# Both output projections of a decoder layer, formed from seven products of half size

## The chip, the cores and the metric

The program runs on one core of a Trainium2 chip. The metric is the device time of one execution in microseconds (us); a kernel's time is the median of its runs.

## The reference

One decoder layer works on x, 1024 tokens by 1024 features in float32. Four steps follow one another, each with a residual and a LayerNorm:

```
x <- LN1(alpha*x + 1/2 * SwiGLU_1(x))
x <- LN2(alpha*x + concat[HGRN2(x), SGU(x)] @ w_out)
x <- LN3(alpha*x + attention(x, LN_m(mem)) @ xa_w_o)
x <- LN4(alpha*x + 1/2 * SwiGLU_2(x))
```

SwiGLU is `(silu(x @ w_gate) * (x @ w_up)) @ w_down` with 2816 inner features. The two products that this case is about are those with `w_out` and with `xa_w_o`: each multiplies a 1024 x 1024 matrix of activations by a 1024 x 1024 weight.

## The kernel before

**Products.** The work is tiled by 128: eight token tiles, eight k-tiles (of the contraction), and halves of 512 tokens or 512 columns. A float32 operand is split into two parts of a shorter float type: `split` has ScalarE copy the high part, and VectorE subtract it from the operand for the low part (L110). `mm3` then makes each product as three matmuls of 128x512, high by high (L131), high by low (L132) and low by high (L133); The activations that a stage multiplies stand transposed, features on the partitions, in four tiles: `xh` and `xl`, high and low, one pair for each half of the tokens.

**The output projections.** `down_group` (L226) computes a group of token tiles: (0, 1), then (2, 3, 4), then (5, 6, 7). A token tile needs two banks, one for each 512 columns. For each of eight k-tiles a group loads 128 rows of the weight, splits them and multiplies, so the weight is loaded and split three times, 24 loads and 24 splits for each projection. A group has 96 or 144 matmuls, the projection 384. When a group ends, `residual_norm` (L214) is started for each of its tiles: it loads the residual, adds the banks onto it (L220), norms the row on VectorE (two halves of statistics, an aggregate, two passes of 128x1024; the reciprocal root on GpSimd), stores the result, and transposes it into `xh` and `xl` for the next stage.

**Order.** Such later work is a coroutine: `spawn` starts it, it yields a time in us, and `tick` goes on with it once so much time of other products has been issued; `drain` ends all of them. So the norms and transposes of a group stand among the matmuls of the next group or stage. In the mixers (L1056 to L1066) the first group is issued, then the last part of the second half of the tokens (`m1.tail()`, four token tiles of the gate's product, whose transposes complete the second half of the mixers' output), then a drain, then the other two groups. Behind them the attention's first query projection (`paq0`, all of the first half's tokens) begins. In the attention the first group of `xa_w_o` is dealt out among the heads of the second half of the tokens, and the other two groups follow; behind them FFN 2 multiplies its first pair of feature tiles. For FFN 2 the transposed output is also kept in float32 (`keep`, tiles `xf_xa`), because FFN 2 forms combinations of it.

**Buffers and engines.** Weights pass through pools of 3 (raw), 6 (high) and 5 (low) buffers; larger temporary tiles come from one pool of 22 of 128x1024; PSUM has six banks for products and two for transposes. A scheduler sets each engine's order when the program is built, and each engine then works through its own queue in that order. SP issues the transfers.

## Time and profile before

| what | value |
|---|---|
| three runs | 2034.47, 2040.79 (the median) and 2042.2 us |
| span of the profiled execution | 2032.8 us |
| TensorE (PE) busy | 2015.5 us in 9646 matmuls |
| VectorE (DVE) busy | 1504.1 us in 2246 instructions |
| ScalarE (ACT) busy | 890.0 us in 1239 instructions |
| GpSimd (POOL) busy | 102.5 us in 144 instructions |

The profiled execution is one of its own; its span, from its first instruction to its last, is the only time known of it, and stands 8.0 us below the median of the three runs.

The profile gives, for each engine, the time in which it is busy; the rows by stretch give the same between two moments of the span, with the granted TensorE clock and the share in which the transfers ran. Matmuls are pipelined, so that one's duration reaches into the next one's; what a matmul takes of TensorE's time is the distance between two starts. A row of one instruction gives start, duration, engine, line, operation, output <- inputs (without buffer numbers) and shapes.

### The profile page before, as it was taken

The page shows a single profiled execution, that of the slowest core. Times are in us where ns is not written, and L with a number is a line of the kernel's source. Part 1 is how long each engine was busy: PE and PEld are TensorE (multiplying, and loading weights), DVE is VectorE, ACT ScalarE, POOL GpSimd, SP SyncE. Part 2 cuts the span into 40 slices and gives each one's busy share as a digit, 9 for nine tenths or more (in the row PEclk, how much of TensorE's full clock was granted, in tenths as well). Part 3 has the DMA queues.
Part 4 walks back from the last instruction along what each step waited for, and adds up shares of the span by engine and source line. Part 5 has one row for each costly group of instructions (what it writes and reads, how often), then busy time and mean ns, then how long its engine had stood idle before and what let it go on. Part 6 is the DMA issues. An engine that isn't in the chain of part 4 may idle for free.

```text
span 2032.8 us, 25339 instructions
## 1 busy us (share of the span) xinstructions
PE 2015.5 (99%) x9646; PEld 1689.1 (83%) x9646; DVE 1504.1 (74%) x2246; ACT 890.0 (44%) x1239; POOL 102.5 (5%) x144
## 2 busy tenths in 40 slices
PE   8999999999999999999999999999999999999998
PEld 7888888888888888888888888888888888888886
DVE  5987677677668967948796855678776776776688
ACT  6633333334533467547644344444333333344432
POOL 0000000000002010100110100010000000000021
PEclk8999999999999999999999999999999999999999
DMA  8333233237887632123156522353232332378874
GB/s 263 122 114 119 78 114 119 78 119 250 290 289 261 222 116 73 53 63 105 41 176 228 162 88 74 122 197 119 88 126 82 104 127 81 109 249 291 297 254 172
DMA packets 244250, 306.88 MB, mean 151 GB/s; under 512 B 14368, under 2 KB 154272, under 8 KB 244128
## 3 DMA queue, kind: packets, MB, share of 16 engines
q1 hardware_dynamic: 244128, 305.26, 45.3%
q8 instruction: 76, 1.25, 0.2%
q14 instruction: 46, 0.38, 0.1%
HBM read 234.44 MB, written 70.78 MB: 150 GB/s over the span
## 4 chain that ended last, share of the span: by engine, by line
PE 93%; DVE 3%; DMA 2%; POOL 1%; issue 1%; SPq 0%; ACT 0%; POOLq 0%; DVEq 0%; ACTq 0%
PE st_gf L131 7%; PE st_uf L131 7%; PE st_gf L133 7%; PE st_uf L133 7%; PE st_gf L132 7%; PE st_uf L132 7%; PE dp_f L133 6%; PE dp_f L131 6%; PE dp_f L132 6%; PE psl L939 2%; PE acc_xa L131 1%; PE acc_xa L133 1%; PE acc_xa L132 1%; PE paq L131 1%; PE paq L133 1%; PE paq L132 1%
## 5 line engine op out<-in xcount | busy, mean ns | idle before, releaser
L132 PE MATMUL dp_f<-wd_f_l,ah_f 128*128 128x512 f32 x552 | 213.3, 390 | 0.0
L131 PE MATMUL dp_f<-wd_f_h,ah_f 128*128 128x512 f32 x552 | 208.4, 390 | 0.0
L133 PE MATMUL dp_f<-wd_f_h,al_f 128*128 128x512 f32 x552 | 206.1, 390 | 0.1
L133 PEld LDWEIGHTS dp_f<-wd_f_h,al_f 128*128 128x128 f32 x552 | 103.7, 188 | 22.2 <-DVE al_f L110 0.9
L132 PEld LDWEIGHTS dp_f<-wd_f_l,ah_f 128*128 128x128 f32 x552 | 103.6, 188 | 21.6
L131 PEld LDWEIGHTS dp_f<-wd_f_h,ah_f 128*128 128x128 f32 x552 | 103.6, 188 | 21.2
L109 ACT ACTIVATE wd_f_h<-wd_f_r 128x1024 fp32r<-128x1024 f32 x72 | 73.2, 1022 | 97.7 <-DVE wd_f_r L436 28.3
L110 DVE TENSOR_TENSOR al_f<-ar_f,ah_f 128x1024 fp32r<-128x1024 f32 x72 | 84.5, 1174 | 24.5 <-ACT ah_f L109 23.6
L109 ACT ACTIVATE ah_f<-ar_f 128x1024 fp32r<-128x1024 f32 x72 | 73.3, 1019 | 59.2 <-DMA ar_f<-lops 54.3
L110 DVE TENSOR_TENSOR wd_f_l<-wd_f_r,wd_f_h 128x1024 fp32r<-128x1024 f32 x72 | 84.3, 1175 | 12.5 <-ACT wd_f_h L109 12.2
L316 DVE TENSOR_TENSOR top_uf<-bot_uf,st_uf 128x512 f32<-128x512 f32 x21 | 14.4, 686 | 81.8 <-PE st_uf L133 81.8
L315 ACT ACTIVATE bot_gf<-st_gf 128x512 f32<-128x512 f32 x21 | 12.5, 597 | 137.1 <-PE st_gf L133 137.1
L560 POOL TENSOR_SCALAR nm_f<-nm_f 128x1 f32<-128x1 f32 x8 | 10.7, 1336 | 1198.8 <-ACT xl L559 1198.8
L131 PE MATMUL st_gf<-xh,wg_f_h 128*128 128x512 f32 x168 | 65.4, 389 | 0.0
L133 PE MATMUL st_gf<-xh,wg_f_l 128*128 128x512 f32 x168 | 65.4, 389 | 0.0
L131 PE MATMUL st_uf<-xh,wu_f_h 128*128 128x512 f32 x168 | 65.4, 389 | 0.0
L132 PE MATMUL st_uf<-xl,wu_f_h 128*128 128x512 f32 x168 | 65.4, 389 | 0.0
L133 PE MATMUL st_uf<-xh,wu_f_l 128*128 128x512 f32 x168 | 65.4, 389 | 0.0
L132 PE MATMUL st_gf<-xl,wg_f_h 128*128 128x512 f32 x168 | 65.3, 389 | 0.0
L109 ACT ACTIVATE wg_f_h<-wg_f_r 128x1024 fp32r<-128x1024 f32 x44 | 46.4, 1056 | 36.2 <-PE st_gf L132 29.3
L109 ACT ACTIVATE wu_f_h<-wu_f_r 128x1024 fp32r<-128x1024 f32 x44 | 46.3, 1053 | 35.7 <-issue 27.2
L110 DVE TENSOR_TENSOR wu_f_l<-wu_f_r,wu_f_h 128x1024 fp32r<-128x1024 f32 x44 | 53.6, 1219 | 3.2 <-PE acc_xa L132 3.2
(456 smaller groups left out, 5960.1 us busy)
## 6 DMA issues: line engine op xcount, KB each, us to landing
ar_f<-lops SPq DMA_DIRECT2D x66, 512.0 KB, 5.0
wd_f_r<-in_ffn_w_down_dram SPq DMA_DIRECT2D x56, 512.0 KB, 4.8
wg_f_r<-in_ffn_w_gate_dram SPq DMA_DIRECT2D x44, 512.0 KB, 3.8
wu_f_r<-in_ffn_w_up_dram SPq DMA_DIRECT2D x44, 512.0 KB, 3.8
wd_mx_r<-in_w_out_dram SPq DMA_DIRECT2D x24, 512.0 KB, 3.6
wd_xa_r<-in_xa_w_o_dram SPq DMA_DIRECT2D x24, 512.0 KB, 3.5
lops<-bot_gf SPq DMA_DIRECT2D x21, 512.0 KB, 2.7
lops<-top_uf SPq DMA_DIRECT2D x21, 512.0 KB, 2.8
```

Source lines behind the costliest of these rows:

```text
L109: order(nc.scalar.activation(hi, src, AF.Copy))
L110: order(nc.vector.tensor_tensor(lo, src, hi.bitcast(F32), op=ALU.subtract))
L131: nc.tensor.matmul(ps, lh, rh, start=first, stop=False)
L132: nc.tensor.matmul(ps, lh, rl, start=False, stop=False)
L133: nc.tensor.matmul(ps, ll, rh, start=False, stop=last)
L315: nc.scalar.activation(b0, product(1), AF.Copy)
L316: nc.vector.tensor_tensor(t0, b0, product(2), op=ALU.add)
L560: nc.gpsimd.tensor_scalar(nmean, nmean, -1.0 / D, None, op0=ALU.mult)
L939: nc.tensor.matmul(psl[:m, (i * NC2 + c) * 64:(i * NC2 + c + 1) * 64] .rearrange("p (n b) -> p n b", b=B), e[:, :m], blk(e, B)[:, :, 1, :] ...
```

## The change

`square` takes the place of `down_group` and `residual_norm` for both projections. It halves the tokens (rows of blocks), the contraction and the columns, and forms the product of the resulting 2x2 blocks from seven products of blocks instead of eight. With a11, a12, a21, a22 for the activations' blocks (first index: half of the tokens, second: half of k) and w11 to w22 for the weight's:

```
t1 = w12 - w11    t2 = w22 - t1    s1 = a21 + a22    s2 = s1 - a11
p1 = a11 w11      p2 = a12 w21     p5 = s1 t1        p6 = s2 t2
p3 = (a12 - s2) w22    p7 = (a11 - a21)(w22 - w12)    p4 = a22 (w21 - t2)
top left  = p1 + p2              top right    = p1 + p6 + p5 + p3
bottom left = p1 + p6 + p7 + p4  bottom right = p1 + p6 + p7 + p5
```

The products run in the order 1, 2, 5, 6, 3, 7, 4. Each has four token tiles and four k-tiles, 48 matmuls, so a projection has 336. Products 1 and 2 end in the banks `sx`, 5 and then 3 are accumulated in `sz`, and 6, 7 and 4 in `sy`; `mm3` got an argument for a bank that is accumulated on after it was read. `top` and `bot` are the residuals of the first and second four token tiles, onto which the banks are added one after the other (`onto`). VectorE forms the weight's combinations (`right`) and the activations' (`plus`), and the operands that are not blocks of the input are split again. The norms of the tiles of `top` are started after product 3, those of `bot` tile by tile in product 4, and `square` ends by completing the coroutines of `top` at once.

Since combinations need the float32 blocks, the mixers and the attention now write their transposed output to float32 tiles (`oa`, `ao`). For the first half of the tokens it is also split into `xh` and `xl`, stored to DRAM, and loaded again (`mx_again`, `ao_again`) when products 5, 6 and 3 need it. In the mixers, `m1.tail()` now comes ahead of the whole projection, four steps of the projection (products 1 and 2) are issued behind it, then the drain, then the rest; in the attention, products 1 and 2 are dealt out among the heads. 

```diff
-    def mm3(ps, lh, ll, rh, rl, first, last):
+    def mm3(ps, lh, ll, rh, rl, first, last, more=False):
...
+    def square(w, left, res_src, gb, bb, dst, name, keep=None):
+        wv = w.rearrange("(kb n i p) (db d) -> kb n db p i d", kb=2, n=2, i=2, p=P, db=2)
+        early = []
+        def block(kb, db, n, of):
+            return load_raw(wv[kb, n, db], f"w{of}_{name}_{n}")
+        def kept(kb, db, n, of):
+            return load_raw(wv[kb, n, db], f"w{of}_{name}_{n}", gt)
+        def plus(a, b, op, o=None):
+            nc.vector.tensor_tensor(a if o is None else o, a, b, op=op)
+            return a if o is None else o
+        t1, t2, b22 = {}, {}, {}
+        def right(p, n):
+            if p == 1:
+                r = block(0, 0, n, p)
+            elif p == 2:
+                r = block(1, 0, n, p)
+            elif p == 5:
+                r = kept(0, 1, n, p)
+                t1[n] = plus(r, block(0, 0, n, "5b"), ALU.subtract)
+            elif p == 6:
+                b22[n] = kept(1, 1, n, p)
+                t2[n] = r = plus(b22[n], t1[n], ALU.subtract, t1[n])
+            elif p == 3:
+                r = b22[n]
+            elif p == 7:
+                r = block(0, 1, n, p)
+                plus(b22[n], r, ALU.subtract, r)
+            else:
+                r = plus(block(1, 0, n, p), t2[n], ALU.subtract)
+            return split_w(r, f"w{p}_{name}_{n}")
+        def product(p, bank, slot, first, done=None):
+            half, k0 = slot
+            ops = [right(p, 0)]
+            def part(t, n):
+                ts = slice(t * P, (t + 1) * P)
+                rh, rl = ops[n]
+                for i in range(2):
+                    k = k0 + 2 * n + i
+                    mm3(bank[t], xh[half][:, k, ts], xl[half][:, k, ts], rh[:, i, :], rl[:, i, :],
+                        first and n == 0 and i == 0, n == 1 and i == 1, not first)
+            if done is None:
+                for n in range(2):
+                    if n == 0:
+                        ops.append(right(p, 1))
+                    for t in range(4):
+                        part(t, n)
+                    yield 5.4
+                return
+            ops.append(right(p, 1))
+            for t in range(4):
+                for n in range(2):
+                    part(t, n)
+                done(t)
+                yield 2.7
+        def residual(tt):
+            r = gt(f"r_{name}_{tt}", (P, 2, HALF))
+            nc.sync.dma_start(r, res_src[tt * P:(tt + 1) * P, :].rearrange("p (h d) -> p h d", h=2))
+            return r
+        def onto(r, acc, scale=None):
+            if scale is None:
+                nc.vector.tensor_tensor(r, r, acc, op=ALU.add)
+            else:
+                nc.vector.scalar_tensor_tensor(r, r, scale, acc, op0=ALU.mult, op1=ALU.add)
+        def norm(r, tt, lag):
+            y = r.rearrange("p h d -> p (h d)")
+            layer_norm(y, gb, bb, f"{name}_{tt}")
+            nc.sync.dma_start(dst[tt * P:(tt + 1) * P, :], y)
+            yield lag
+            yield from to_xT_steps(y, tt, list(range(KT)), f"{name}_{tt}", keep, 2.6)
+        x = [ps_mm(f"sx_{name}_{t}") for t in range(4)]
+        yield from product(1, x, (0, 0), True)
+        p1 = [gt(f"p1_{name}_{i}", (P, 2, HALF)) for i in range(2)]
+        p1 = [p1[t // 2][:, t % 2, :] for t in range(4)]
+        for t in range(4):
+            nc.scalar.activation(p1[t], x[t], AF.Copy)
+        yield from product(2, x, (0, 4), False)
+        top = [residual(t) for t in range(4)]
+        for t in range(4):
+            onto(top[t][:, 0], x[t], ALPHA)
+        s1, a11, a12, a21, a22 = {}, {}, {}, {}, {}
+        for n in range(2):
+            a21[n], a22[n] = left(1, 0, n), left(1, 1, n)
+            s1[n] = plus(a21[n], a22[n], ALU.add, gt(f"s1_{name}_{n}", (P, 2, HALF)))
+            ks = slice(2 * n, 2 * n + 2)
+            split(s1[n], xh[1][:, ks, :], xl[1][:, ks, :])
+        z = [(ps_tr if t > 1 else ps_mm)(f"sz_{name}_{t}") for t in range(4)]
+        yield from product(5, z, (1, 0), True)
+        for n in range(2):
+            a11[n] = left(0, 0, n)
+            ks = slice(2 * n, 2 * n + 2)
+            plus(a11[n], a21[n], ALU.subtract, a21[n])
+            plus(s1[n], a11[n], ALU.subtract)
+            split(s1[n], xh[0][:, ks, :], xl[0][:, ks, :])
+        for t in range(4):
+            onto(top[t][:, 1], p1[t], ALPHA)
+        bot = [residual(4 + t) for t in range(4)]
+        for t in range(4):
+            onto(bot[t][:, 1], z[t], ALPHA)
+        y = [ps_mm(f"sy_{name}_{t}") for t in range(4)]
+        yield from product(6, y, (0, 0), True)
+        for n in range(2):
+            ks = slice(4 + 2 * n, 6 + 2 * n)
+            a12[n] = left(0, 1, n)
+            plus(a12[n], s1[n], ALU.subtract)
+            split(a12[n], xh[0][:, ks, :], xl[0][:, ks, :])
+        for t in range(4):
+            onto(top[t][:, 1], y[t])
+            onto(bot[t][:, 0], p1[t], ALPHA)
+        yield from product(3, z, (0, 4), False)
+        for n in range(2):
+            ks = slice(2 * n, 2 * n + 2)
+            split(a21[n], xh[1][:, ks, :], xl[1][:, ks, :])
+        for t in range(4):
+            onto(top[t][:, 1], z[t])
+            early.append(norm(top[t], t, 6 + 4.5 * t))
+            spawn(early[-1])
+            onto(bot[t][:, 1], p1[t])
+        yield from product(7, y, (1, 0), False)
+        for n in range(2):
+            ks = slice(4 + 2 * n, 6 + 2 * n)
+            split(a22[n], xh[1][:, ks, :], xl[1][:, ks, :])
+        for t in range(4):
+            onto(bot[t][:, 1], y[t])
+        def done(t):
+            onto(bot[t][:, 0], y[t])
+            spawn(norm(bot[t], 4 + t, 8))
+        yield from product(4, y, (1, 4), False, done)
+        for f in [f for f in flows if f[0] in early]:
+            flows.remove(f)
+            for _ in f[0]:
+                pass
...
+            cs = slice(i * P, (i + 1) * P)
+            for j in range(2):
+                if i == 0:
+                    self.oa[j] = gt(f"oaT{self.half}{j}", (P, 2, HALF))
+                nc.scalar.activation(self.oa[j][:, :, cs], ptv[:, 2 * j:2 * j + 2, :], AF.Copy)
+            if self.half:
+                return
+            split(ptv, xh[0][:, 0:4, cs], xl[0][:, 0:4, cs])
             if i == NC2 - 1:
                 for j in range(2):
                     ks = slice(4 + 2 * j, 6 + 2 * j)
-                    split(self.u[j], xh[self.half][:, ks, :], xl[self.half][:, ks, :])
+                    split(self.u[j], xh[0][:, ks, :], xl[0][:, ks, :])
+                    nc.sync.dma_start(oa_dram[0, j], self.oa[j])
+                    nc.sync.dma_start(oa_dram[1, j], self.u[j])
...
-    def mix_group(grp):
-        return down_group(a["w_out"][0], KT, grp, xT_operand, res[0], gb, bb, res[1], "mx")
-    run(mix_group((0, 1)))
+    def mixed(i, j, n):
+        if i:
+            return (m1.u if j else m1.oa)[n]
+        a32 = gt(f"mx_again_{j}{n}", (P, 2, HALF))
+        nc.sync.dma_start(a32, oa_dram[j, n])
+        return a32
+    project = square(a["w_out"][0], mixed, res[0], gb, bb, res[1], "mx")
     play(m1.tail())
+    for _ in range(4):
+        tick(next(project))
     drain()
-    run(mix_group((2, 3, 4)))
-    run(mix_group((5, 6, 7)))
+    run(project)
...
+        ao = gt(f"ao{half}_{h}", (P, 2, HALF))
         for j in range(2):
             c = h * 2 + j
             cs = slice(c * P, (c + 1) * P)
...
-            split(ps, xh[half][:, c, :], xl[half][:, c, :])
+            nc.scalar.activation(ao[:, j, :], ps, AF.Copy)
+        if half:
+            aos[h] = ao
+        else:
+            split(ao, xh[0][:, 2 * h:2 * h + 2, :], xl[0][:, 2 * h:2 * h + 2, :])
+            nc.sync.dma_start(ao_dram[h], ao)
...
+    project = square(a["xa_w_o"][0], attended, res[1], gb, bb, res[2], "xa", xf2)
     for h in range(H):
         if h:
-            next(first)
+            tick(next(project))
         probs_T(1, h)
         if h < H - 1:
             scores(1, h + 1)
         else:
-            next(first)
-        next(first)
+            tick(next(project))
         attend(1, h)
-    run(first)
-    run(out_group((2, 3, 4)))
-    run(out_group((5, 6, 7)))
+    run(project)
```

The first place is VectorE's queue in the mixers' projection, where the last tile of the second half of the mixers' output (`ot11`) has been gated. Before, there stood the gating, the splits of normed tiles of the first group (`xl0<-pt_mx`), those of the second group's weights (`wd_mx`) and of the mixers' second half (`xl1<-ut`):

```order
L875 TENSOR_TENSOR ot11_7751<-ot11_7751,sg12_8720 128x512
L110 TENSOR_TENSOR xl0_117<-pt_mx_1_0_8723,xh0_115 128x4x128
L110 TENSOR_TENSOR xl0_117<-pt_mx_1_4_8730,xh0_115 128x4x128
L110 TENSOR_TENSOR wd_mx_2_1_l_8830<-wd_mx_2_1_r_8827,wd_mx_2_1_h_8829 128x1024
L110 TENSOR_TENSOR wd_mx_2_2_l_8854<-wd_mx_2_2_r_8851,wd_mx_2_2_h_8853 128x1024
L110 TENSOR_TENSOR wd_mx_2_3_l_8878<-wd_mx_2_3_r_8875,wd_mx_2_3_h_8877 128x1024
L110 TENSOR_TENSOR xl1_118<-ut10_7433,xh1_116 128x1024
```

In the changed kernel, after s1 has been formed and split, the residuals `r_mx`, the bank of products 1 and 2 (`sx`), the kept product 1 (`p1`), the combinations for product 5 (`w5`) and those of the activations (`oaT`, reloaded as `mx_again`) stand in this order:

```order
L296 SCALAR_TENSOR_TENSOR r_mx_3_8739<-r_mx_3_8739,sx_mx_3_8541 128x512
L296 SCALAR_TENSOR_TENSOR r_mx_3_8739<-r_mx_3_8739,p1_mx_1_8638 128x512
L235 TENSOR_TENSOR w5_mx_0_r_8757<-w5_mx_0_r_8757,w5b_mx_0_r_8759 128x1024
L235 TENSOR_TENSOR w5_mx_1_r_8766<-w5_mx_1_r_8766,w5b_mx_1_r_8768 128x1024
L235 TENSOR_TENSOR oaT10_8708<-mx_again_00_8823,oaT10_8708 128x1024
L235 TENSOR_TENSOR s1_mx_0_8745<-s1_mx_0_8745,mx_again_00_8823 128x1024
L235 TENSOR_TENSOR oaT11_8710<-mx_again_01_8829,oaT11_8710 128x1024
L235 TENSOR_TENSOR s1_mx_1_8749<-s1_mx_1_8749,mx_again_01_8829 128x1024
L296 SCALAR_TENSOR_TENSOR r_mx_4_8839<-r_mx_4_8839,p1_mx_0_8637 128x512
L110 TENSOR_TENSOR w5_mx_0_l_8763<-w5_mx_0_r_8757,w5_mx_0_h_8762 128x1024
L296 SCALAR_TENSOR_TENSOR r_mx_5_8841<-r_mx_5_8841,p1_mx_0_8637 128x512
L110 TENSOR_TENSOR w5_mx_1_l_8772<-w5_mx_1_r_8766,w5_mx_1_h_8771 128x1024
```

The split of product 5's weights (`w5_mx_0_l`) now stands behind residual additions and combinations for product 6.

The second place is TensorE's queue between the end of the mixers' projection and the first query projection (`paq0`). Before, one followed the other (`acc_mx` are the banks of the projection):

```order
L131 MATMUL acc_mx_7_1_9048<-wd_mx_5_7_h_9261,xh1_116 128x512
L132 MATMUL acc_mx_7_1_9048<-wd_mx_5_7_l_9262,xh1_116 128x512
L133 MATMUL acc_mx_7_1_9048<-wd_mx_5_7_h_9261,xl1_118 128x512
L131 MATMUL paq0_0_9361<-xh0_115,waq0_0_h_9357 128x512
L132 MATMUL paq0_0_9361<-xl0_117,waq0_0_h_9357 128x512
L133 MATMUL paq0_0_9361<-xh0_115,waq0_0_l_9358 128x512
```

Now (`pt_mx_t_j` are the transposes of half j of token tile t of the projection's normed output, four to a row):

```order
L159 MATMUL pt_mx_2_4_9245<-ident_75,r_mx_2_8737 128x128 x4
L159 MATMUL pt_mx_4_0_9252<-ident_75,r_mx_4_8839 128x128 x4
L159 MATMUL pt_mx_3_0_9284<-ident_75,r_mx_3_8739 128x128 x4
L132 MATMUL paq0_0_9342<-xh0_115,waq0_0_h_9338 128x512
L132 MATMUL paq0_1_9398<-xh0_115,waq0_1_h_9394 128x512
L132 MATMUL paq0_2_9445<-xh0_115,waq0_2_h_9441 128x512
L132 MATMUL paq0_3_9480<-xh0_115,waq0_3_h_9476 128x512
L132 MATMUL paq0_4_9513<-xh0_115,waq0_4_h_9509 128x512
L132 MATMUL paq0_5_9548<-xh0_115,waq0_5_h_9544 128x512
L159 MATMUL pt_mx_4_4_9291<-ident_75,r_mx_4_8839 128x128 x4
L159 MATMUL pt_mx_5_0_9298<-ident_75,r_mx_5_8841 128x128 x4
L133 MATMUL paq0_0_9342<-xl0_117,waq0_0_h_9338 128x512
```

Transposes of four tiles, and six matmuls on high parts alone, now stand ahead of the first matmul on a low part, which needs tiles 0 to 3 normed and split.

The third place is the same queue between the attention's projection and FFN 2 (`pg_f2` and `pu_f2` are its first products). Before:

```order
L131 MATMUL acc_xa_7_1_11048<-wd_xa_5_7_h_11289,xh1_116 128x512
L132 MATMUL acc_xa_7_1_11048<-wd_xa_5_7_l_11290,xh1_116 128x512
L133 MATMUL acc_xa_7_1_11048<-wd_xa_5_7_h_11289,xl1_118 128x512
L131 MATMUL pg_f2_0_0_11366<-xh0_115,wg_f2_0_h_11362 128x512
L132 MATMUL pg_f2_0_0_11366<-xl0_117,wg_f2_0_h_11362 128x512
L133 MATMUL pg_f2_0_0_11366<-xh0_115,wg_f2_0_l_11363 128x512
```

Now:

```order
L159 MATMUL pt_xa_2_0_11177<-ident_75,r_xa_2_10681 128x128 x4
L159 MATMUL pt_xa_2_4_11213<-ident_75,r_xa_2_10681 128x128 x4
L159 MATMUL pt_xa_4_0_11224<-ident_75,r_xa_4_10783 128x128 x4
L159 MATMUL pt_xa_3_0_11262<-ident_75,r_xa_3_10683 128x128 x4
L159 MATMUL pt_xa_4_4_11273<-ident_75,r_xa_4_10783 128x128 x4
L132 MATMUL pg_f2_0_0_11315<-xh0_115,wg_f2_0_h_11311 128x512
L132 MATMUL pu_f2_0_0_11379<-xh0_115,wu_f2_0_h_11375 128x512
L132 MATMUL pg_f2_1_0_11435<-xh0_115,wg_f2_1_h_11431 128x512
L132 MATMUL pu_f2_1_0_11466<-xh0_115,wu_f2_1_h_11462 128x512
L159 MATMUL pt_xa_5_0_11286<-ident_75,r_xa_5_10785 128x128 x4
L159 MATMUL pt_xa_3_4_11297<-ident_75,r_xa_3_10683 128x128 x4
L133 MATMUL pg_f2_0_0_11315<-xl0_117,wg_f2_0_h_11311 128x512
```

Here too the transposes of tiles 2 to 5 and four matmuls on high parts stand between the projection and the first low part.

52 lines of the change are left out of this document (18 added, 34 removed).

## The prediction

> **What bounds the kernel now.** I read the page's busy table and its chain of waits first, then stretches around the two projections, then single instructions there.
>
> ```profile
> span 2032.8 us, 25339 instructions
> PE 2015.5 (99%) x9646; PEld 1689.1 (83%) x9646; DVE 1504.1 (74%) x2246; ACT 890.0 (44%) x1239; POOL 102.5 (5%) x144
> PE 93%; DVE 3%; DMA 2%; POOL 1%; issue 1%; SPq 0%; ACT 0%; POOLq 0%; DVEq 0%; ACTq 0%
> 1020.00:1060.00 40.00, 39.58 (x238) 34.32 (x236) 37.20 (x89) 19.35 (x27) 3.62 (x6) 1.00 0.57 196
> 1060.00:1100.00 40.00, 40.00 (x210) 33.99 (x209) 27.14 (x39) 16.07 (x29) 4.13 (x5) 1.00 0.54 202
> 1100.00:1150.00 50.00, 50.00 (x234) 41.58 (x233) 38.39 (x45) 20.95 (x23) 5.40 (x6) 1.00 0.60 196
> 1150.00:1190.00 40.00, 40.00 (x191) 33.35 (x190) 30.15 (x40) 13.59 (x19) 3.46 (x6) 1.00 0.42 132
> sum 170.00, PE 169.58 PEld 143.24 DVE 132.87 ACT 69.95 POOL 16.62; mean PE 42.39 PEld 35.81 DVE 33.22 ACT 17.49 POOL 4.15
> sum 125.00, PE 125.00 PEld 104.74 DVE 92.42 ACT 52.89 POOL 13.62; mean PE 41.67 PEld 34.91 DVE 30.81 ACT 17.63 POOL 4.54
> ```
>
> The first three lines are the page's: TensorE is busy 99% of the span and makes 93% of the chain. The others give busy time by stretch (PE, PEld, DVE, ACT, POOL, then the clock). The mixers' projection with its surroundings is 1020 to 1190: PE lost 0.42 us there, and VectorE, the next in line, was free for 170 - 132.9 = 37.1 us. The last line sums 1275 to 1400, around the attention's projection: PE lost nothing, VectorE was free for 32.6 us. So every matmul that goes shortens the run, as long as VectorE keeps up.
>
> **What the change removes.** Each projection had 384 matmuls and now has 7/8 of them, 336; the instruction order shows 96 fewer over the program. Their price is the distance between starts, not the 0.39 us that one takes:
>
> ```profile
> 1101.78 0.39 PE L131 MATMUL acc_mx<-wd_mx_h,xh 128*128 128x512 f32 x1
> ...
> 1107.90 0.39 PE L131 MATMUL acc_mx<-wd_mx_h,xh 128*128 128x512 f32 x1
> 1068.80 0.87 PE pt_mx L158 x8
> ```
>
> From the first to the last of these rows there are 27 starts in 6.12 us: 0.2267 us each. The removal is worth 96 x 0.2267 = **21.8 us**, all of it on the path. A transpose costs 0.87 / 8 = 0.109 us.
>
> **What it adds.** By the order, VectorE gets 34 more instructions of 128x1024 and 20 more of 128x512. Their prices are again distances between starts, from stretches in which VectorE did not pause:
>
> ```profile
> 1154.03 1.22 DVE L110 TENSOR_TENSOR waq_l<-waq_r,waq_h 128x1024 fp32r<-128x1024 f32 x1
> 1155.16 0.68 DVE L220 SCALAR_TENSOR_TENSOR r_mx<-r_mx,acc_mx 128x512 f32<-128x512 f32 x1
> 1155.76 0.20 DVE L196 BATCH_NORM_AGGREGATE mv_mx<-st_mx 128x2 f32<-128x12 f32 x1
> 1156.00 1.28 DVE L202 SCALAR_TENSOR_TENSOR r_mx<-r_mx,mv_mx,g_mx 128x1024 f32<-128x1024 f32 x1
> 1157.20 1.28 DVE L192 BATCH_NORM_STATS2 st_mx<-r_mx 128x6 f32<-128x512 f32 x2
> 1158.40 1.27 DVE L204 SCALAR_TENSOR_TENSOR r_mx<-r_mx,rs_mx,b_mx 128x1024 f32<-128x1024 f32 x1
> 1159.58 1.22 DVE L110 TENSOR_TENSOR waq_l<-waq_r,waq_h 128x1024 fp32r<-128x1024 f32 x1
> ...
> 1420.31 1.22 DVE L270 TENSOR_TENSOR xf_xa<-xf_xa,xf_xa 128x1024 f32<-128x1024 f32 x1
> 1421.45 1.22 DVE L110 TENSOR_TENSOR xc6l_f<-xf_xa,xc6h_f 128x1024 fp32r<-128x1024 f32 x1
> 1428.85 0.68 DVE L286 TENSOR_TENSOR wu_f_sa<-wu_f_sa,wu_f_r 128x512 f32<-128x512 f32 x1
> 1429.45 0.69 DVE L287 TENSOR_TENSOR wu_f_r<-wu_f_r,wu_f_r 128x512 f32<-128x512 f32 x1
> 1400.81 1.43 DVE L110 TENSOR_TENSOR xl<-xf_xa,xh 128x256 fp32r<-128x256 f32 x4
> 1402.15 0.68 DVE L285 TENSOR_TENSOR wg_f_sa<-wg_f_r 128x512 f32<-128x512 f32 x1
> ```
>
> A plain 128x1024 operation costs 1.13 to 1.14 us, a 128x512 one or half of the statistics 0.60, the LayerNorm's 128x1024 steps 1.20 and 1.18 (I take 1.19), the aggregate 0.24, a 128x256 split 1.34 / 4 = 0.335. The addition is 34 x 1.135 + 20 x 0.60 = 50.6 us, 25.3 for each projection. By totals that would just fit: 37.1 - 10.9 = 26.2 us are left free at the mixers. But VectorE works in order, so what counts is what stands in its queue between the moment when s1 can be formed and the moment when the next stage has its operand. I count rows of the order.
>
> At the **mixers**, the queue from s1_mx_0 to the split of pt_mx_3_0 (xl for the first k-tiles of the fourth token tile, which the first query projection reads whole) holds 119 instructions: 43 plain 128x1024 (48.8 us), 58 of 128x512 or statistics (34.8), 6 aggregates (1.4), 12 LayerNorm steps (14.3), **99.3 us** together. On the way, the low part of product 5's first weights comes after 18.5 us and that of product 6's after 34.5 us. TensorE has little to put there. After the last transposes of the mixers' output it has 240 matmuls of products 5, 6, 3, 7 and 4 (54.4 us), 40 transposes (4.4) and six matmuls that need only high parts (1.4), 60.2 us. Before the change the same place was covered: the first query projection followed the last accumulation directly, since tiles 0 to 3 were normed while the last group was multiplied. Now all eight tiles end in the last three products, and behind them the queue still holds the norms; r_mx_4 of the lower half stands ahead of r_mx_3's transposes. ScalarE's last copies for s1 delay the start by about 1 us (an estimate: seven copies, at the 384 ns that the tile's copies take in the row below, less the 1.7 us of transposes beside them). TensorE idles 99.3 + 1.0 - 60.2 = **40.1 us**.
>
> ```profile
> L172 ACT ACTIVATE xf_xa<-pt_xa x32: 362/384/408, 1329.3 to 1411.4; 128x256 f32<-128x256 f32 x32
> ```
>
> At the **attention** the queue from s1_xa_1 to the split that lets FFN 2's first product go on holds 39 plain 128x1024 (44.3), 50 of 128x512 or statistics (30.0), 7 aggregates (1.7), 12 LayerNorm steps (14.3) and 15 of 128x256 (5.0): 95.3 us. TensorE has 54.4 + 44 transposes (4.8) + four matmuls (0.9) = 60.1. With the same 1.0 us of lead it idles **36.2 us**.
>
> Does VectorE itself pause there? I went through the releases: product 6 ends some 45 us after s1 at the latest, its first addition stands after 50; products 7 and 4 follow at about 64 and 75 us, their additions stand at 64 to 79. Margins are 0 to 10 us, so a late product adds a few us. ScalarE's extra splits and copies cost nothing: it is busy 70 of 170 us. Neither do transfers: 24 weight loads become 14, with four reloads and four stores beside them.
>
> **The clock.** An idle TensorE does not come back at full speed. The run's start shows it (clock in the third column from the right):
>
> ```profile
> 8.00:10.00 2.00, 0.44 (x2) 0.20 (x2) 0.00 (x0) 1.70 (x2) 1.01 (x3) 1.00 1.03 369
> 10.00:12.00 2.00, 0.87 (x6) 0.64 (x6) 0.89 (x2) 1.41 (x2) 0.00 (x0) 0.86 1.14 339
> 12.00:14.00 2.00, 1.09 (x4) 0.72 (x4) 1.38 (x3) 1.23 (x2) 0.00 (x0) 0.50 1.00 392
> 16.00:18.00 2.00, 2.00 (x10) 2.00 (x11) 2.00 (x5) 0.63 (x1) 0.00 (x0) 0.50 1.16 332
> 20.00:22.00 2.00, 2.00 (x12) 2.00 (x11) 2.00 (x4) 0.00 (x0) 0.00 (x0) 0.58 1.01 399
> 22.00:24.00 2.00, 2.00 (x19) 2.00 (x18) 0.92 (x2) 0.63 (x1) 0.00 (x0) 1.00 1.18 244
> ```
>
> After some us of gaps the clock was 0.50, and it stayed there from 16, when the gaps ended, to about 21.5. That is 5.5 us at half speed, 2.7 us lost. Slowed matmuls inside the two stretches fall into gaps; the two resumptions are on the path: **5.4 us** (between 0, if the transposes keep the clock up, and some 10, if the queues slip too). The Trainium skill ("TensorE: Matmul & The Clock Gate", Part 1) says that the clock halves after an idle window of about 3.4 us and doubles after a busy one as long; the rows agree on the half, and by its window the two would cost 3.4 us, by the rows 5.4.
>
> **The sum:** 40.1 + 36.2 + 5.4 - 21.8 = +59.9 us. The span goes from 2032.8 to 2092.7. The three times shown are 2034.5, 2040.8 and 2042.2, so the median lies 8.0 above the profiled span, and I forecast **2101 us** for the median.
>
> **Rivals.** (a) *VectorE hides it, faster.* One mechanism: its free 69.7 us take the 50.6, so PE stays the bound and the 21.8 us are won: 2019 us. It decides by one point, whether the split of pt_mx_3_0 comes some 60 us after s1 rather than 99. The totals speak for it, the counted queue against it: 0.06. (b) *Only the ends show.* Operands are ready in time and TensorE waits just from the end of product 4 to that split, about 20 us in the queue (8 tiles' worth of norms and splits behind the last addition). Both ends: 2 x 20 + 5.4 - 21.8 = +23.6, 2064 us, 0.06; one end: about 2042, 0.03. Against it stands w5's place, behind ten residual and operand steps. (c) *More is lost.* VectorE pays the whole duration of each instruction (1.22, 0.68, 1.28 us in the rows above) instead of the distance: the queues become 108.7 and 105.3 us, +19.3 us, 2120; waits for loads or for slowed products could cost as much. Against it, starts in the rows lie before the earlier ends: 0.10. The Trainium skill ("VectorE: DVE Perf Modes", The DRAIN you can't avoid) has this rule, that the next operation waits until the pipe is empty; the rows disagree by about 0.08 us an instruction.
>
> **Numbers.** The forecast, VectorE bound at both places, has 0.75. Unknown lead, clock and margins make it 2085 to 2115; with (c) the range reaches to 2128, and a little of the way to (b), 2082. Left out are (a), (b) and the end of (c), under 0.2. About 0.5%, 10 us, is what a measurement here can tell from no change: faster 0.06 from (a), same 0.03 from (b) with one end, slower 0.91.
>
> **What would show it.** Right: TensorE's busy share falls to about 95%; idle stretches of 15 to 20 us just before product 5 and some 20 us before the first query projection and FFN 2's first product, put down to VectorE's splits; VectorE above 95% busy for about 100 us in each; the clock at 0.5 after the gaps; 96 matmuls fewer at the same 0.227 us. Wrong: no gaps and PE at 99% (then a); gaps only at the ends (b); VectorE pausing inside the stretches, or its starts 1.2 us apart (c).

## The result and the profile after

The changed kernel takes 2094.32 us (median of four runs, 2094.28 to 2097.16), against 2038.22 us (four runs, 2034.47 to 2042.2): a ratio of 1.0283, with a 95% interval of 1.0264 to 1.0302. It is slower, as forecast. The profiled span is 2092.6 us; the prediction's sum gave 2092.7. Spans are compared below, and before's span belongs to a fast execution: in every run whose span is on record the time stands 1.7 us above it, so 2032.8 us goes with 2034.5, the lowest of before's four times. By the medians the change costs 56.1 us, by the two spans 59.8.

The page's busy table and its chain of waits:

```profile
PE 2009.8 (96%) x9550; PEld 1680.1 (80%) x9550; DVE 1552.0 (74%) x2300; ACT 901.9 (43%) x1265; POOL 101.6 (5%) x144
PE 87%; DVE 6%; DMA 2%; issue 2%; ACT 1%; POOL 1%; SPq 1%; POOLq 0%; DVEq 0%; ACTq 0%
```

TensorE makes 96 matmuls fewer but is busy only 5.7 us less (2015.5 to 2009.8), where 96 x 0.2267 = 21.8 us were removed: 16.1 us went into matmuls that are recorded longer, as those that run at half speed in the rows further below, or that no next one overlaps. Its idle time grew from 17.3 to 82.8 us. So 65.5 + 16.1 - 21.8 = 59.8 us, the whole difference of the spans. VectorE's part of the chain grew from 3% to 6%.

Where this lies is seen by stretch (length, then busy time of PE, PEld, DVE, ACT and POOL, the granted clock, DMA share and GB/s). The last two rows are the two queues counted in the prediction, from s1's first operation to the end of the split that releases the next stage:

```profile
1060.00:1080.00 20.00, 20.00 (x102) 17.00 (x101) 4.57 (x11) 3.54 (x12) 1.20 (x2) 1.00 0.57 213
1080.00:1100.00 20.00, 5.48 (x26) 3.69 (x24) 15.84 (x19) 7.71 (x13) 0.00 (x0) 0.66 0.57 194
1100.00:1120.00 20.00, 14.69 (x54) 11.48 (x55) 20.00 (x21) 11.68 (x12) 0.00 (x0) 0.83 0.28 88
...
1160.00:1180.00 20.00, 7.11 (x35) 5.85 (x34) 19.89 (x28) 5.49 (x8) 6.11 (x7) 0.62 0.40 134
1084.20:1184.00 99.80, 67.19 (x277) 54.11 (x278) 98.84 (x119) 33.32 (x37) 8.91 (x12) 0.80 0.41 136
1349.50:1444.40 94.90, 66.24 (x281) 53.28 (x282) 94.83 (x125) 34.95 (x60) 11.05 (x14) 0.84 0.41 141
```

VectorE is busy 99% and 100% of the two queues, while over the whole span it is busy 74%. From 1060 to 1080, just ahead, it was busy 4.6 of 20 us: it waited for the mixers' last tile, at the end 7.55 us for ScalarE's copies of it (the row of 1084.16 further below). TensorE fell to 5.5 of 20 us before product 5 and to 7.1 of 20 before the query projection.

TensorE's waits at the mixers (the first five rows) and at the attention (the other three), as tile and line, what released it, total us, times, longest:

```profile
PE sz_mx L132 <- ACT w_mx_h L109: 12.8, 1, 12.8
PE pt_mx L159 <- issue: 10.3, 2, 7.5
PE sz_mx L133 <- DVE w_mx_l L110: 4.2, 1, 4.2
PE pt_mx L159 <- DVE xl L110: 2.6, 1, 2.6
...
PE paq L132 <- ACT xh L109: 0.7, 1, 0.7
...
PE sz_xa L132 <- ACT w_xa_h L109: 13.0, 1, 13.0
PE pt_xa L159 <- DVE mv_xa L197: 9.6, 1, 9.6
PE sz_xa L133 <- DVE w_xa_l L110: 4.3, 1, 4.3
```

Two groups of waits at each place carry 57.5 of the 65.5 us: 12.8 + 4.2 = 17.0 and 13.0 + 4.3 = 17.3 us for product 5's weights, and 10.3 + 2.6 + 0.7 = 13.6 and 9.6 us ahead of the next stage. The first of each pair is put down to ScalarE, but ScalarE was busy 7.7 of 20 us there: it copies what VectorE combines, and so stands behind VectorE. (At the mixers, its copy of `w_mx_h` began at 1095.36, after 7.7 us of waiting for VectorE's combination.) The 10.3 us ahead of the query projection are put down to "issue", that is, to nothing that the profile shows. The single rows show what was waited for: the transposes start 0.1 us after VectorE's last LayerNorm step on a tile of `r_mx` has ended, here at 1169.66 and again at 1179.09, with the transposes at 1179.19.

```profile
1168.39 1.27 DVE L205 SCALAR_TENSOR_TENSOR r_mx<-r_mx,rs_mx,b_mx 128x1024 f32<-128x1024 f32 x1
1169.76 1.94 PE L159 MATMUL pt_mx<-ident,r_mx 128*128 128x128 f32 x8 [2.85 <-issue]
```

### The profile page after: what moved, and what is told of

It is laid out like the page before. It is cut to its first block, busy times and chain, and to the rows that moved or that the text cites. A ratio compares the mean times of both kernels' runs of the same rounds, so it can differ in the third digit from the quotient of the medians.

```text
span 2092.6 us, 25192 instructions
## 1 busy us (share of the span) xinstructions
PE 2009.8 (96%) x9550; PEld 1680.1 (80%) x9550; DVE 1552.0 (74%) x2300; ACT 901.9 (43%) x1265; POOL 101.6 (5%) x144
## 4 chain that ended last, share of the span: by engine, by line
PE 87%; DVE 6%; DMA 2%; issue 2%; ACT 1%; POOL 1%; SPq 1%; POOLq 0%; DVEq 0%; ACTq 0%
PE st_uf L134 6%; PE st_uf L133 6%; PE st_uf L132 6%; PE st_gf L134 6%; PE st_gf L133 6%; PE st_gf L132 6%; PE dp_f L132 6%; PE dp_f L134 6%; PE dp_f L133 6%; PE psl L1077 2%; PE paq L132 1%; PE paq L134 1%; PE paq L133 1%; DVE xl L110 1%; PE ps_wu L132 1%
## 5 line engine op out<-in xcount | busy, mean ns | idle before, releaser
L110 DVE TENSOR_TENSOR wg_f_l<-wg_f_r,wg_f_h 128x1024 fp32r<-128x1024 f32 x44 | 53.6, 1218 | 0.2 <-ACT wg_f_h L109 0.2
```

The costliest lines, as they stand in the source:

```text
L110: order(nc.vector.tensor_tensor(lo, src, hi.bitcast(F32), op=ALU.subtract))
```

## The experiments

The theory under test, called **A** in the expectations, is the prediction's: at each place the time is that of VectorE's queue between the moment when s1 can be formed and the moment when the next stage has its operand, whatever waits lie inside.

Whole spans can't be compared to a few us, since the code ahead of the change, which is the same in all kernels, ended between 1018.4 and 1025.8 us. Where it was late, the down projection of the first FFN had waited, as in the run with the change in the mixers alone:

```profile
PE dp_f L132 <- DVE db_f L737: 2.9, 1, 2.9
```

So I compare pieces, between the last starts of three groups of matmuls: `ps_wvs` (end of the code ahead), `paq` (end of the query projections, behind the mixers) and `dp_f` (end of FFN 2). A row of such a group has shortest, median and longest duration in ns, then first and last start. Before, then after:

```profile
L133 PE MATMUL ps_wvs<-wvs_h,xl x64: 389/389/478, 813.8 to 1019.9; 128*128 128x512 f32 x64
L133 PE MATMUL paq<-xh,waq_l x128: 389/389/398, 1153.3 to 1265.6; 128*128 128x512 f32 x128
L133 PE MATMUL dp_f<-wd_f_h,al_f x552: 387/389/504, 493.4 to 2023.7; 128*128 128x512 f32 x184
...
L134 PE MATMUL ps_wvs<-wvs_h,xl x64: 389/390/477, 814.5 to 1020.7; 128*128 128x512 f32 x64
L134 PE MATMUL paq<-xh,waq_l x128: 387/390/477, 1186.0 to 1297.3; 128*128 128x512 f32 x128
L134 PE MATMUL dp_f<-wd_f_h,al_f x552: 387/390/504, 494.2 to 2083.6; 128*128 128x512 f32 x184
```

From `ps_wvs` to `paq` is called **mixers** here, from `paq` to `dp_f` **rest** (attention and FFN 2). The rest holds the down projection of FFN 2, which waits in some executions as the first FFN's does; the last column has the sum of these waits. All times in us:

| kernel | time | span | mixers | rest | waits in FFN 2 |
|---|---|---|---|---|---|
| before | 2038.22 (4 runs) | 2032.8 | 245.7 | 758.1 | 0.0 |
| after | 2094.32 (4 runs) | 2092.6 | 276.6 | 786.3 | 2.2 |
| mixers alone | 2075.9 | 2074.2 | 278.4 | 761.4 | 2.5 |
| attention alone | 2067.57 | 2065.9 | 245.2 | 786.0 | 0.0 |
| product 5's weights first | 2098.31 (4 runs) | 2094.5 | 277.2 | 787.5 | 0.9 |
| ten more in each queue | 2119.23 | 2117.5 | 288.5 | 800.3 | 0.0 |
| product 5's weights ahead of s1 | 2085.27 | 2083.6 | 272.3 | 783.9 | 0.8 |
| statistics on ScalarE | 2094.11 | 2092.4 | 277.9 | 780.9 | 0.6 |
| combinations on GpSimd | 2109.46 | 2107.8 | 281.0 | 792.4 | 1.3 |
| these three together | 2088.68 | 2086.9 | 273.2 | 784.6 | 1.4 |
| filled gap | 2091.59 | 2089.9 | 276.0 | 784.7 | 0.2 |
| halves exchanged (first) | 2064.02 | 2062.2 | 254.3 | 773.6 | 0.4 |
| halves exchanged (second) | 2062.32 | 2060.6 | 255.0 | 775.4 | 1.4 |
| the second, timed | 2069.64 (4 runs) | 2066.7 | 258.6 | 777.7 | 4.2 |

Times without a count are of a single run, and span and pieces are those of one execution each. The last two rows are the same kernel: its two executions differ by 3.6 us in the mixers and 2.3 in the rest, so a difference of this size between single runs shows little by itself. Line numbers in rows of an experiment are those of its own code, a few lines off.

### One projection at a time

One projection gets the old groups back, first the attention's, then the mixers':

```diff
-    project = square(a["xa_w_o"][0], attended, res[1], gb, bb, res[2], "xa", xf2)
+    def out_group(grp):
+        return down_group(a["xa_w_o"][0], KT, grp, xT_operand, res[1], gb, bb, res[2], "xa", xf2)
+    first = out_group((0, 1))
...
```

> Only the mixers' projection is formed from seven products; the attention's is as before. If VectorE's queue is the bound at each place by itself (theory A), this costs the mixers' share of what the changed kernel's trace shows between its markers, about 31 us: a span near 2064 us. If the loss is one event that both projections share (a clock that is never recovered, a delay that only shows in the last stage; theory B), the span lies near 2033 or near 2093.

> Only the attention's projection is formed from seven products. Theory A: the other share, about 28 us: a span near 2061 us, and the two spans' losses add up to that of the whole change (59.8). Theory B: near 2033 or 2093.

The two spans came out 10 and 5 us longer than A's numbers, but for the most part not at the change: the mixers cost 278.4 - 245.7 = 32.7 us and the attention 786.0 - 758.1 = 27.9, against 30.9 and 28.2 in the whole change. The code ahead ended 5.6 and 5.9 us later than in before, and with the mixers alone FFN 2's down projection waited 2.5 us. So each place loses its own 28 to 33 us, and neither needs the other for it.

### The order of waits inside the queue

TensorE's largest waits are those for product 5's weights. In this run the residuals of `top` stand behind these weights instead of ahead of them:

```diff
-        top = [residual(t) for t in range(4)]
-        for t in range(4):
-            onto(top[t][:, 0], x[t], ALPHA)
...
             plus(s1[n], a11[n], ALU.subtract)
             split(s1[n], xh[0][:, ks, :], xl[0][:, ks, :])
+        top = [residual(t) for t in range(4)]
+        for t in range(4):
+            onto(top[t][:, 0], x[t], ALPHA)
```

> The same instructions, but the additions of products 1 and 2 onto the upper residuals stand behind product 5's operands. By the instruction order VectorE's queue from s1 to the split that the query projection needs stays at 99 us, and product 5's first low part comes 8 us after s1 is begun instead of 17 to 18. Theory A (the queue's sum counts, wherever the waits fall): the wait in front of product 5 shrinks by about 8 us, the wait at the end grows by as much, and the time stays within 5 us of the changed kernel's. Theory C (product 5's late operand is the loss, the end is only its echo): about 8 us for each projection come back, 2078 us.

The groups of low parts of product 5 and of the query projection in this run, then its waits:

```profile
L133 PE MATMUL sz_mx<-w_mx_l,xh x32: 387/389/797, 1094.8 to 1143.5; 128*128 128x512 f32 x32
L133 PE MATMUL paq<-xl,waq_h x128: 389/389/775, 1186.1 to 1297.8; 128*128 128x512 f32 x128
...
PE sz_mx L132 <- ACT w_mx_h L109: 6.3, 1, 6.3
PE sz_mx L133 <- DVE w_mx_l L110: 2.5, 1, 2.5
PE sz_mx L132 <- ACT xh L109: 6.5, 1, 6.5
PE sy_mx L132 <- ACT w_mx_h L109: 5.6, 1, 5.6
```

Product 5 got its low parts 8 us earlier (1094.8 against 1102.8 in the timeline further below), and the query projection started at 1186.1 against 1185.7. TensorE waited 6.3 + 2.5 = 8.8 us for product 5's weights instead of 17.0. The 8.2 us did not go to the end, as expected, where the waits shrank from 13.6 to 10.9 us: they came back as 5.6 us before product 6 (`sy_mx`) and as the 6.5 us for `xh`, which stand before product 3, in the same banks `sz`. The time is a ratio of 1.0292 to before (1.0266 to 1.0319), about that of the change itself. The longest wait of this stretch, which another engine bounds, was worth nothing by itself.

### Ten operations more

Each queue gets ten more operations of 128x1024, a repeated subtraction whose result is not changed by it:

```diff
             split(s1[n], xh[1][:, ks, :], xl[1][:, ks, :])
+            for _ in range(5):
+                nc.vector.tensor_tensor(xl[1][:, ks, :], s1[n], xh[1][:, ks, :].bitcast(F32), op=ALU.subtract)
```

> Each low part of s1 is formed six times instead of once, ten more 128x1024 operations on VectorE for each projection, spread over the first 30 us of its queue; TensorE gets nothing more to do. Theory A: each costs its 1.135 us, 11.4 us for a projection and 22.7 together: a span near 2115 us. If VectorE has room between s1 and the end (theory D: loads, ScalarE or the banks set the pace), less than half of it, under 2104 us.

The mixers took 11.9 us more, where 10 x 1.135 gives 11.4, and the rest 14.0, or 16.2 without FFN 2's waits. So an instruction in these queues costs its full distance at the end. The surplus in the attention is partly VectorE's own pause, for product 3 (start, duration, operation, tiles; in brackets the idle time ahead of it and who ended it):

```profile
1427.16 1.22 DVE L110 TENSOR_TENSOR w_xa_l<-w_xa_r,w_xa_h 128x1024 fp32r<-128x1024 f32 x1 [2.76 <-PE sz_xa L133]
```

The low parts of weights have five buffers, and this split had to wait until product 3 had read one of them. The prediction's margins of 0 to 10 us were those of the additions; this wait stood in none of its terms.

### Ten operations fewer, in three ways

**Product 5's weights ahead of s1.** The combinations and splits of product 5's weights need no activations. They move from the queue into product 2, when VectorE is nearly free:

```diff
-            ops = [right(p, 0)]
+            ops = [made.pop((p, 0), None) or right(p, 0)]
...
-        yield from product(2, x, (0, 4), False)
+        second = product(2, x, (0, 4), False)
+        yield next(second)
+        for n in range(2):
+            made[5, n] = right(5, n)
+        yield from second
```

> Product 5's right operands (two combinations and two splits for each projection) are formed between products 1 and 2, where the changed kernel's VectorE is idle for over 10 us, instead of behind s1. VectorE's queue from s1 to the next stage's first low part falls from 99.3 to 94.8 us at the mixers and from 95.2 to 90.7 at the attention. Theory A (the queue's sum counts): 4.5 us come back at each place. Theory C (product 5's late operand is the loss): product 5 starts over 10 us earlier, and as much comes back at each place.

The span fell by 9.0 us, as expected of it, but by 4.3 in the mixers and only 2.4 in the rest, of which FFN 2's waits are 1.4; 2.3 are the code ahead. So the two places gave some 5 us, and the agreement is in good part chance. In the attention VectorE paused three times for products, 3.2 us in all, the longest (2.71 us, at 1394.40) again for a weight's low buffer that product 3 held.

**Statistics on ScalarE.** The norm's means and squares move to ScalarE, with the scaling on GpSimd:

```diff
-            layer_norm(y, gb, bb, f"{name}_{tt}")
...
+                nc.scalar.activation(y, y, AF.Copy, accum_out=nmean)
+                nc.gpsimd.tensor_scalar(nmean, nmean, -1.0 / D, None, op0=ALU.mult)
+                nc.scalar.activation(junk, y, AF.Square, bias=nmean, accum_out=ss)
+                rsqrt_eps(rs, ss, 1, n, scale=1.0 / D)
...
```

> The mean and the sum of squares of all eight tiles' rows are formed by two passes on ScalarE instead of two statistics and an aggregate on VectorE; VectorE keeps the two passes that scale and shift. The queue falls from 99.3 to 94.2 us and from 95.2 to 86.4. Theory A: 5 and 9 us come back. Theory G (the chain of a tile's norm, which now goes ScalarE, GpSimd, ScalarE, GpSimd, VectorE, sets the end): nothing comes back or the time grows.

VectorE's own work fell (1552.0 to 1532.8 us over the span), yet the mixers took 1.3 us more; the rest took 5.4 less, of which FFN 2's waits are 1.6. Expected were 5 and 9 us less. In the norm, VectorE now waits for ScalarE, and ScalarE for GpSimd:

```profile
1161.51 1.15 ACT L307 ACTIVATE junk<-r_mx,nm_mx 128x1024 f32<-128x1024 f32 x1 [0.89 <-POOL nm_mx L306]
1162.79 1.28 DVE L309 SCALAR_TENSOR_TENSOR r_mx<-r_mx,nm_mx,g_mx 128x1024 f32<-128x1024 f32 x1 [0.80 <-ACT junk L307]
```

VectorE paused seven times for ScalarE in the mixers, some 4.5 us, about what it had been relieved of (5.1 by the count of the queue). Work moved off the bounding engine helped little where it lay on the way from one of its instructions to the next.

**Combinations on GpSimd.** Products 6, 7 and 4 take their weights' combinations from GpSimd:

```diff
-                t2[n] = r = plus(b22[n], t1[n], ALU.subtract, t1[n])
+                t2[n] = r = gplus(b22[n], t1[n], ALU.subtract, t1[n])
...
```

> Six of the eight weight combinations of each projection (for products 6, 7 and 4) are formed on GpSimd instead of VectorE. The queue falls by 6.8 us at each place. Theory A: 6.8 us come back at each, provided that a combination on GpSimd takes no more than some 4 us, which no trace shows yet, and that VectorE's own instructions keep their distances beside it. Theory H (the two engines disturb one another): VectorE's 128x1024 operations become longer than 1.135 us apart while GpSimd works, and little or nothing comes back.

It cost 4.4 us in the mixers and 6.1 in the rest. First the two groups of GpSimd's operations (x6, busy us, mean ns), then an operation of VectorE beside them:

```profile
L239 POOL TENSOR_TENSOR w_mx_r<-w_mx_r 128x1024 f32<-128x1024 f32 x6 | 28.1, 4701 | 40.3 <-DMA w_mx_r<-in_w_out_dram 31.1 <-DVE w_mx_l L110 9.2
L239 POOL TENSOR_TENSOR w_xa_r<-w_xa_r 128x1024 f32<-128x1024 f32 x6 | 30.8, 5153 | 186.1 <-DMA w_xa_r<-in_xa_w_o_dram 186.1
...
1098.30 2.23 DVE L300 SCALAR_TENSOR_TENSOR r_mx<-r_mx,p_mx 128x512 f32<-128x512 f32 x1
```

GpSimd takes 4.7 to 5.2 us in the mean for an operation that takes VectorE 1.22, and VectorE beside it took 2.23 us where a 128x512 took 0.68. The operands come late: at 1117.68 VectorE paused 3.39 us for ScalarE's copy of a weight, which had waited 8.15 us for GpSimd. And the bounding engine is itself slowed: over the span it was busy 1552.0 us, as in the change, with 12 operations fewer, so that the 12 x 1.135 = 13.6 us it was relieved of went into slower ones.

**All three together:**

> The three edits together: product 5's operands early, statistics on ScalarE, six combinations on GpSimd. The queue is 81.7 us at the mixers and 76.2 at the attention, 17.6 and 19.0 less. Theory A: 36 us come back, a span near 2056 us, still slower than before the change. If chains take over (theory G), it stops short of that, at 2070 or more.

The span fell by 5.7 us instead of 36. The longest waits now stand before product 6, 12.0 + 7.2 us at the mixers and 3.6 + 14.9 at the attention:

```profile
PE sy_xa L133 <- DVE w_xa_l L110: 14.9, 1, 14.9
```

GpSimd formed five combinations there from 1357.43 to 1375.09, and five of VectorE's operations beside them took 2.2 to 3.4 us. Which of the three edits cost how much of the 30 us was not tried.

### A filled gap

Is the slow clock after a wait on the path? 130 transposes fill the first wait, so that TensorE does not rest:

```diff
+        for i in range(130):
+            nc.tensor.transpose(z[3][:, (i % 4) * P:(i % 4 + 1) * P], ident, ident)
         yield from product(5, z, (1, 0), True)
```

> Ahead of product 5 TensorE makes 130 transposes of the identity into a bank that product 5 then overwrites, so that it works through the first wait (14 us of work in a wait of 12.8). Theory A (VectorE's queue sets the end; matmuls at half speed inside the stretch fall into waits): product 5's first matmuls run at full speed, and the time from the arrival of the second half to the query projection stays within 1 us. Theory K (the low clock after a wait is on the path, as the prediction's term of 2.7 us for a resumption has it): up to 2.7 us come back at each place. If the transposes outlast the wait, they cost up to 1.5 us instead.

The transposes and the matmuls behind them:

```profile
1083.44 14.41 PE L324 MATMUL sz_mx<-ident 128*128 128x128 f32 x130 [0.19 <-ACT oaT L1014]
1102.33 0.50 PE L133 MATMUL sz_mx<-w_mx_l,xh 128*128 128x512 f32 x1 [3.55 <-DVE w_mx_l L110]
1102.97 0.63 PE L132 MATMUL sz_mx<-w_mx_h,xh 128*128 128x512 f32 x1
1106.32 0.40 PE L133 MATMUL sz_mx<-w_mx_l,xh 128*128 128x512 f32 x1
```

The mixers took 276.0 us against 276.6; the rest took 784.7 against 786.3, but FFN 2's waits are 2.0 us less. From the end of the last transposes (at the attention, of its output's matmuls) to the first low part of the next stage are 101.3 us against 102.0, and 96.7 against 96.6. The wait of 3.55 us that was left slowed the matmuls again, to 0.63 us each, so the fill did not keep the clock up throughout. It removed most of the idle time there, and neither end moved by 1 us: what TensorE loses in this part of the queue, resting or slowed, is off the path.

### The halves exchanged

The queues are long because five of seven products wait for the last tokens. If the blocks of the first tokens are taken as the second row, products 5 and 4 and the operands s1, t1, t2 need first tokens only, and VectorE can form them while it is idle. The products then run in the order 5, 4, then 1, 2, 6, 7, 3; products 1, 6 and 7 are accumulated in one bank, which saves additions. The queue between the last tokens and the next stage shrinks from 99.3 and 95.2 us to 68.5 and 66.4 by count. Both versions also hold back the splits of the attention's keys and values, four operations (4.5 us) of the mixers' queue in the change. (The second version issues three steps of the projection rather than four ahead of the drain, and holds back loads of the query weights.)

```diff
-        x = [ps_mm(f"sx_{name}_{t}") for t in range(4)]
-        yield from product(1, x, (0, 0), True)
+        e = [ps_mm(f"se_{name}_{t}") for t in range(4)]
+        yield from product(5, e, (0, 0), True)
...
+        yield from product(4, e, (0, 4), True)
...
+        yield from product(1, x, (1, 0), True)
...
-        yield from product(4, y, (1, 4), False, done)
+        yield from product(3, v, (1, 0), True, done3)
```

> The seven products with the halves of the tokens exchanged: the rows that s1, p5 and p4 need are now the first half, which is there some hundred us earlier. So p5 and p4 take the place of p1 and p2 ahead of the second half's arrival, and their operands, s1 and four combinations are made while VectorE is idle; behind the arrival stand p2, p1, p6, p7 and p3 in the order of the queue. p1 + p6 and p6 + p7 are accumulated in PSUM, which saves additions; the splits of the attention's keys and values wait until a late tile of the mixers is normed. By the instruction order the queue behind the arrival holds 68.5 us at the mixers and 66.4 at the attention instead of 99.3 and 95.2, against about 60 of TensorE. Theory A: TensorE waits 9 and 7 us instead of 41 and 37, and 21.8 us of matmuls are gone: a span near 2028 to 2036 us, that of the kernel before or a little under. Theory G (chains of several engines take over when the queue is short): 2045 or more.

> The same, but the last transposes of the mixers' second half are issued five matmuls ahead of the end of p4 instead of behind it, and the loads of the third to eighth query weights wait until a tile of the mixers is normed. Theory A: the queue at the mixers begins 1 us earlier and is 1 us shorter: 1 to 3 us less than the run before it. Theory G: no difference.

> The exchanged halves again, timed against the kernel before. By its profile 2060 to 2064 us, 1.2 to 1.4% slower than before; theory A holds that TensorE's waits for VectorE are the rest of it, so it is not faster than before in any round.

Of the change's 59.8 us, 30.4 and 32.0 came back, and 25.9 by the span of the timed runs: the largest effect of all runs, and mainly one of the dependencies, since VectorE makes only two instructions fewer. TensorE is busy again where it had stopped for product 5, 19.2 of 20 us against 5.5 (second version, columns as above):

```profile
1080.00:1100.00 20.00, 19.18 (x93) 15.84 (x92) 17.26 (x25) 9.72 (x23) 1.20 (x2) 1.00 0.84 323
```

It is still slower than before: timed, 2069.64 us (2064.94 to 2074.51), above the 2060 to 2064 expected, a ratio of 1.0148 (1.0117 to 1.0179), or 1.5%, clear of the noise. By count, the queues exceed TensorE's 60.2 us by only 8.3 and 6.2, less than the 21.8 removed. So theory A had the span at 2028 to 2036 us and was at least 26 us off: it says where the time of the change itself lies, not what bounds a kernel with queues as short as these. What is left are many small waits, the largest group in the attention:

```profile
PE pt_xa L159 <- DVE r_xa L205: 8.2, 2, 5.7
```

TensorE was busy 2011.7 us there, 18.0 above the 1993.7 that before's matmuls less 21.8 would take, and idle 48.9: 31.6 + 18.0 - 21.8 = 27.8 us, the distance of this span from that of before. How much of the 18.0 us is on the path in this version wasn't tried. No kernel of these runs beats the one before.

## Why the prediction was right

Its mechanism was right: VectorE's in-order queue sets the time at both places, and its length was counted to 0.5 us. One term of the sum, the clock's, was wrong, and the sum came out within 0.1 us only because other small terms happened to replace it; that closeness is luck.

**The removal** held: 9646 became 9550 matmuls, and full-speed starts are still 0.23 us apart (rows of 1186.02 to 1186.25 below).

**The addition** held: 54 instructions more on VectorE, and 47.9 us more of busy time where 50.6 were counted in distances.

**The two queues**, the step that carries the forecast, held to 0.5 us. Counted were 99.3 and 95.3 us; the windows above took 99.8 and 94.9, the first with the very 119 instructions counted, the second with 125 instead of 123; in the first VectorE paused 0.85 us. On the way, product 5's first low part was ready 18.5 us after s1's start, as counted (1101.51 + 1.14 against 1084.16):

```profile
1084.16 2.36 DVE L235 TENSOR_TENSOR s_mx<-oaT,ut 128x1024 f32<-128x1024 f32 x2 [7.55 <-ACT oaT L1012]
1101.51 1.23 DVE L110 TENSOR_TENSOR w_mx_l<-w_mx_r,w_mx_h 128x1024 fp32r<-128x1024 f32 x1
1182.83 1.28 DVE L110 TENSOR_TENSOR xl<-pt_mx,xh 128x512 fp32r<-128x512 f32 x2
...
1082.50 1.21 PE L1006 MATMUL pt_oa<-ident,ot 128*128 128x128 f32 x8 [0.31 <-ACT oaT L1012]
1102.79 0.79 PE L133 MATMUL sz_mx<-w_mx_l,xh 128*128 128x512 f32 x1 [4.25 <-DVE w_mx_l L110]
1103.38 0.63 PE L134 MATMUL sz_mx<-w_mx_h,xl 128*128 128x512 f32 x1
1103.81 0.63 PE L132 MATMUL sz_mx<-w_mx_h,xh 128*128 128x512 f32 x1
1106.79 0.39 PE L134 MATMUL sz_mx<-w_mx_h,xl 128*128 128x512 f32 x1
1184.54 1.40 PE L159 MATMUL pt_mx<-ident,r_mx 128*128 128x128 f32 x8
1185.70 0.48 PE L133 MATMUL paq<-xl,waq_h 128*128 128x512 f32 x1
1186.02 0.40 PE L134 MATMUL paq<-xh,waq_l 128*128 128x512 f32 x1
1186.25 0.39 PE L132 MATMUL paq<-xh,waq_h 128*128 128x512 f32 x1
1445.31 0.47 PE L133 MATMUL pg_f<-xl,wg_f_h 128*128 128x512 f32 x1
```

**The two idle terms** were close: from the end of the last transposes (1083.71) to the first low part of the query projection (1185.70) are 102.0 us, less TensorE's 60.2 gives 41.8 (forecast 40.1). At the attention, from the end of its output's matmuls (1348.70) to 1445.31 are 96.6, so 36.5 (36.2). The lead was 0.4 and 0.8 us instead of 1.0. The first low part of the query projection followed 1.6 us behind the end of the split (1184.11), since the eight transposes of 1184.54 stood ahead of it.

**The clock's 5.4 us** were wrong as a term, and the sum was kept by others. The term put both slow resumptions behind the split. But at the two ends TensorE had matmuls on high parts and transposes to go through before it, and they took up the slow phase while VectorE was still at work: behind the split, starts are 0.23 us apart almost at once (1186.02, 1186.25; at the attention 1445.62, 1445.86). Only the eight transposes behind it were slowed on the path, 1.2 and 1.0 us instead of 0.87. In place of the 5.4 us came, by chance, 2.0 us of the idle terms, 0.8 us of the code ahead, and 2.2 us that I had not foreseen, waits in FFN 2's down projection:

```profile
PE dp_f L132 <- DVE db_f L706: 1.4, 1, 1.4
PE dp_f L134 <- DVE al_f L110: 0.8, 1, 0.8
```

So 41.8 + 36.5 + 0.8 + 2.2 - 21.8 = 59.5, against 59.8 measured.

**The median** came 6.7 us lower than forecast. Its whole error is the 8.0 us added for before's median over its profile; here the median stands 1.7 us above. Before's offset came from one execution with a short span, not from something to be carried over: within an execution the time is 1.7 us above the span.

**What would show it:** TensorE at 96% (about 95), 17.0 and 17.3 us before product 5 (15 to 20), VectorE above 95%, the clock at 0.50 after the gaps (in stretches of 2 us from 1092 to 1106), all there. The waits before the next stages were shorter, 13.6 and 9.9 us with the small last one rather than some 20; TensorE had lost time on the way in slowed matmuls and small waits, as the 2.0 us before product 3, though these were not added up.

**The rivals** fell: (a), since the queue and not the totals decided; (b), since waits stood at the start too, and moving those alone gave nothing; (c), since VectorE's distances stayed at 1.135 us, by the counted sum above. The Trainium skill's drain ("VectorE: DVE Perf Modes", The DRAIN you can't avoid) did not appear as 0.08 us more an instruction here either.

## What to carry to other kernels

A trade of matmuls for elementwise work is priced in the stretch between its dependencies: count the in-order queue of the engine that receives it, from the moment at which its first input exists to the moment at which the next stage can start, and compare that with TensorE's work in the same stretch; a busy share of 74% over the span says nothing. In such a stretch an earlier operand for the waiting engine was worth nothing here, and operations taken out of the queue gave back less than their distance where another dependency took over. What helped most was to choose which half of the data comes last, so that less of the work depends on it.

## What the runs showed of the hardware

The slow phase of TensorE after a wait can be read from distances between starts. After the wait for product 5's low parts they are 0.43 us from 1103.38 to 1103.81, and full speed is back by 1106.79, 4.0 us after the wait's end; in the filled gap the matmuls of 0.63 us began at 1102.97, and full speed was back at 1106.32, 3.4 us later (4.0 after the wait's end). The clock column agrees once it is read in short stretches: its 0.83 for 1100 to 1120 is 6.8 us at half speed and 13.2 at full. So what the prediction's term got wrong was not the 5.5 us that it read at the run's start but where such a phase falls. The Trainium skill ("TensorE: Matmul & The Clock Gate", Part 1) gives a busy window of about 3.4 us; the 3.4 us in the filled gap agree with it, and the 4.0 and 5.5 us are longer.

GpSimd at work on 128x1024 operands held up some of VectorE's operations beside it: the one of 2.23 us instead of 0.68 ended at 1100.53, just behind GpSimd's operation (1096.03 to 1099.99), while one of 1096.56 had kept its 1.22 us. In sum VectorE lost the 13.6 us that it had been relieved of.
